# Sample-sequence state updates moved from the scan stage to the out-projection stage, with their operands kept in DRAM

## The chip, the cores and the metric

The kernel runs on one core of a Trainium2 chip. The metric is the device time of one execution in microseconds (us). The engines are named as in the profile: PE (TensorE, matrix multiplies; PEld are its weight loads), DVE (VectorE), ACT (ScalarE), POOL (GpSimd) and SP (SyncE, which here only issues DMAs). Each engine works through its own list of instructions in order: an instruction that waits holds everything behind it on that engine.

## The reference

One inference step of a small hybrid decoder, for one prompt of 512 tokens and 8 sampled sequences of 4 new tokens each (544 tokens in all, width 1024). There are two layers. Layer A is a Mamba-2 mixer: an in-projection, a causal convolution, a chunked state-space scan and an out-projection. Layer B is a dilated attention mixer over keys and values shared with a cache. What the change concerns is the state of the sampled sequences in layer A:

```python
def step(s, inp):
    dec, cs = inp
    return dec[..., None, None] * s + cs, s

s_final, s_in = lax.scan(step, s0, (chunk_decay, chunk_states))
y_off = jnp.einsum("bctgn,cbgjpn,bgjct->bctgjp", Cc, s_in, jnp.exp(a_cs))
y = (y_diag + y_off).reshape(b, lp, nh, p)[:, :l]
return y, s_final.reshape(b, nh, p, SSM_STATE)
```

For each of the 8 sampled sequences and each of the 32 heads the old state (64 x 128 fp32, the input `state_ssm`) is used twice: the output `y_off` multiplies it with C, and the new state is decay x old state + B^T (x dt decay), which is an output of the step (`ssm_sample`). All the old states are 8.4 MB, and so are all the new ones. Nothing later in the step reads a new state; it only has to be stored. The output `y` goes on into the gate and the out-projection.

## The kernel before

Matrix multiplies are fp32-accurate: each operand is split into a high and a low part (`whi`/`wlo`, `xh`/`xl`, `vh`/`vl`, `hh`/`hl`), and three passes are summed in PSUM. A projection tile makes 128 output features of all 544 tokens; `pa` holds tokens 0 to 255 of it and `pb` the other 288. Work is emitted in program order and a list scheduler sets each engine's order from it; `tc.high_priority` pulls single instructions ahead.

**Stage A (0 to about 375 us).** The in-projection tiles are a filler that `run(pace)` deals out between the scan's units. The 4 groups of 8 heads have six units each: `ssm_chunk(g, c)` for the prompt's four chunks of 128 tokens and `ssm_quad(g, q)` for two sets of four sampled sequences (the "quads"; Q0 to Q7 in order of group and set). A unit is a generator in two or three parts, so that one unit's operand preparation stands ahead of the part of the unit before that uses it. `ssm_quad` does:
- `s0`: two loads of 512 KB (two sequences each, 128 x 1024) into `s_t`, from a pool of two such buffers, on SP's queue (L685);
- `cbp`, `xp`, `yos`: PE transposes B and x, and multiplies C with the old state (`yos`, four matmuls);
- `xdt`, `xdd`: x times dt, and x times dt and decay, 128 x 512, on DVE;
- `btr`, `xr`: B and `xdd` as high and low parts in different rows of one tile, by `hi_lo_rows` (one ACT at L213 and one DVE at L214 each);
- L723, on POOL: the old state times its decay `dec`, in place, 128 x 512 per sequence;
- `ms`, `yds`, `yot`, `ytmp`: the output of the new tokens, added into `v`;
- `update(j)`: one matmul `up` (K = 32 rows) per sequence, DVE adds it to the decayed state (L744), and after each second sequence ACT's queue stores 512 KB (`ssmS`, L746).

At the end of a group `gate_skip` adds the skip term to `v` and `gate_mul_a` multiplies `v` by the gate `uz` (L592, on POOL for groups 0 to 2 and on DVE for the last) and sums squares (`ssq`, L598). `v_split` then makes `vh` and `vl` of it (L757 ACT, L758 DVE).

**Middle stage (about 375 to 600 us).** The out-projection has 8 tiles, m = 0 to 7, of 96 matmuls each. After a tile's matmuls `h1_tile(m)` scales, adds the residual, makes `hh` and `hl`, squares on ACT (`sqb`) and adds the squares into `hss`, on POOL for m = 1 to 6 (L861). Then one step of the generator `tables` follows, which makes the attention's bias tables: a PE matmul `bvp` per step, whose one-hot operand `oh` comes by DMAs from POOL's queue. After the out-projection come 16 tiles for the shared keys and values (`wkv`), 48 matmuls each. The weights of a tile come in halves (`wraw`, 512 KB each) and are split into `whi` on ACT (L199) and `wlo` on DVE (L200) about a tile ahead.

**Slabs.** Tiles of 128 x 4 x 544 fp32 (8.7 KB a partition) come by `half(...)` from one pool of 13 buffers. In the out-projection 12 are held: four each of `vh` and `vl`, two each of `hh` and `hl`.

**Stage C (about 600 to 963 us)** is the attention, which the change leaves alone.

Of the kernel before, what the change touches and what calls it, by code (L numbers as in the profile page):

```python
# [12 lines left out]
F32 = mybir.dt.float32  # L13
# [14 lines left out]
HP = 64  # L28
NG = 4
# [95 lines left out]
def tile_yoco_step(  # L125
# [16 lines left out]
    def mm(*a, **k):  # L142
        pin(nc.tensor.matmul(*a, **k))  # L143
# [16 lines left out]
    def pss(name, shape=(128, 512)):  # L160
        return psum.tile(list(shape), F32, name=name, tag="ss", bufs=5)
# [50 lines left out]
    def hi_lo_rows(out, src, c, rows=128):  # L212
        nc.scalar.activation(out, src, AF.Copy, scale=hls[0:rows, c + 1:c + 2])  # L213
        nc.vector.scalar_tensor_tensor(out, src, hls[0:rows, c:c + 1], f32(out), op0=ALU.mult, op1=ALU.add)  # L214
# [68 lines left out]
    sed0 = dram.tile([128, 2, 8], F32, name="sed0")  # L283
    sed = dram.tile([2, NH, 32], F32, name="sed")
    vnd = dram.tile([NB, TS, ATH, 128], F32, name="vnd")
    kvd = dram.tile([ATH, 128, T + SEQ], F32, name="kvd")

    def dap(t, off, ap):
# [204 lines left out]
    def spread_decays():  # L493
        dx = pss("dx")
        mm(dx[:, 0:384], ones, dgs.rearrange("p a b -> p (a b)"), start=True, stop=True)
        dv = dx[:, 0:384].rearrange("p (r j h) -> p r j h", r=3, j=4)
        nc.scalar.copy(dec[:, 0:4], dv[:, 0])
        nc.scalar.copy(dec[:, 4:12].rearrange("p (j r) h -> p r j h", r=2), dv[:, 1:3])

    def tok_transposes():  # L500
        spread_decays()
# [38 lines left out]
    def bc(ap, n):  # L540
        return ap[:, :, None].to_broadcast([ap.shape[0], ap.shape[1], n])
# [121 lines left out]
    def ssm_quad(g, q):  # L663
        xs, v, G = xs_t[g], v_t[g], grp[g]
        hs = slice(8 * g, 8 * g + 8)
        if q == 0:
            bp = wk.tile([128, 2, 4, 32], F32, name="bp", bufs=1)
            cp = wk.tile([128, 2, 4, 32], F32, name="cp", bufs=1)
            nc.gpsimd.memset(bp, 0.0)
            thrice(bp.rearrange("p q j c -> p (q j) c"), BT[:, g, SEQ:T])  # L670
            nc.gpsimd.memset(cp, 0.0)
            nc.gpsimd.tensor_copy(cp.rearrange("p q j c -> p (q j) c")[:, :, 0:TS],
                                  CT[:, g, SEQ:T].rearrange("p (b c) -> p b c", c=TS))
            as_ = wk.tile([128, 8, 32], F32, name="as", bufs=1)
            dma(as_, dap(sed, 8 * g * 32, [[0, 128], [32, 8], [1, 32]]))
            es = wk.tile([128, 4, 32], F32, name="es", bufs=1)
            for s in range(2):
                dma(es[64 * s:64 * s + 64], dap(sed, (NH + 8 * g + s) * 32, [[0, 64], [64, 4], [1, 32]]))
            G["smp"] = bp, cp, as_, es
        bp, cp, as_, es = G["smp"]  # L680
        sq_ = slice(16 * q, 16 * q + 16)
        s_t = []
        for jp in range(2):
            s_t.append(wk.tile([128, 2, 512], F32, name="s0", bufs=2))
            dma(s_t[jp], s0[g, :, 4 * q + 2 * jp:4 * q + 2 * jp + 2, :])  # L685
        xpd = wk.tile([128, 4, 4, 32], F32, name="xpd", bufs=1)
        nc.gpsimd.memset(xpd, 0.0)
        for i in range(4):
            thrice(xpd[:, i], xs[:, i, SEQ + 16 * q:SEQ + 16 * q + 16])
        bq = bp[:, q].rearrange("p a b -> p (a b)")  # L690
        cbp = pss("cbp")
        transpose(cbp[:, 128:256], bq, ident)
        mm(cbp[:, 0:16], bq, CT[:, g, SEQ + 16 * q:SEQ + 16 * q + 16], start=True, stop=True)
        xp = pss("xp", (128, 4, 128))
        for i in range(4):
            transpose(xp[:, i, :], xpd[:, i].rearrange("p a b -> p (a b)"), ident)
        yo = pss("yos")
        for j in range(4):
            mm(yo[32 * j:32 * j + 32, :], cp[:, q, j, :], s_t[j // 2][:, j % 2, :], start=True, stop=True)
        bt = wk.tile([128, 128], F32R, name="btr", bufs=1)  # L700
        hi_lo_rows(bt, cbp[:, 128:256], 0)
        cbm = wk.tile([128, 16], F32, name="cbs")
        with tc.high_priority():
            nc.vector.tensor_tensor(cbm, cbp[:, 0:16], smask, op=ALU.mult)
        yos = wk.tile([128, 512], F32, name="yos", bufs=1)
        nc.scalar.copy(yos, yo)
        xph = xp.rearrange("p a (h d) -> p (a h) d", d=HP)
        xdt = wk.tile([128, 8, HP], F32, name="xdt", tag="xd", bufs=3)
        with tc.high_priority():
            nc.vector.tensor_tensor(xdt, xph, bc(tok[:, 4 + q, 1, hs], HP), op=ALU.mult)  # L710
        xdd = wk.tile([128, 8, HP], F32, name="xdd", tag="xd", bufs=3)
        with tc.high_priority():
            nc.vector.tensor_tensor(xdd, xph, bc(tok[:, 4 + q, 2, hs], HP), op=ALU.mult)
        xr = wk.tile([128, 8, HP], F32R, name="xr", bufs=1)
        hi_lo_rows(xr, xdd, 2)
        ms = wk.tile([128, 8, 16], F32, name="ms")
        nc.vector.tensor_tensor(ms, as_[:, :, sq_], bc(tok[:, 4 + q, 0, hs], 16), op=ALU.subtract)
        nc.vector.tensor_scalar(ms, ms, 0.0, None, op0=ALU.min)
        nc.scalar.activation(ms, ms, AF.Exp)
        nc.vector.tensor_tensor(ms, ms, cbm[:, None, :].to_broadcast([128, 8, 16]), op=ALU.mult)  # L720
        for j in range(4):
            sv = s_t[j // 2][:, j % 2, :].rearrange("p (a b) -> p a b", b=HP)
            nc.gpsimd.tensor_tensor(sv, sv, bc(dec[:, 4 + 4 * q + j, hs], HP), op=ALU.mult)  # L723
# [12 lines left out]
        nc.vector.tensor_tensor(v[:, :, SEQ + 16 * q:SEQ + 16 * q + 16], yds,  # L736
                                tmp.rearrange("p i j t -> p i (j t)"), op=ALU.add)

        def update(j):
            up = pss("up", (128, 8, HP))  # L740
            mm(up.rearrange("p a b -> p (a b)"), bt[32 * j:32 * j + 32, :],
               xr[32 * j:32 * j + 32].rearrange("p a b -> p (a b)"), start=True, stop=True)
            sv = s_t[j // 2][:, j % 2, :].rearrange("p (a b) -> p a b", b=HP)
            nc.vector.tensor_tensor(sv, up, sv, op=ALU.add)  # L744
            if j % 2:
                nc.scalar.dma_start(ssmS[g, :, 4 * q + j - 1:4 * q + j + 1, :], s_t[j // 2])  # L746

        for j in range(3):
            update(j)
        yield  # L750
        update(3)

    def v_split(g, i):
        gg = g_gate[:, 4 * g + i:4 * g + i + 1]
# [89 lines left out]
    def h1_tile(m, pa, pb):  # L844
# [15 lines left out]
        nc.scalar.activation(sq, hm, AF.Square)  # L860
        (nc.gpsimd if m < KD - 1 else nc.vector).tensor_tensor(hss, hss, sq, op=ALU.add)  # L861

    def load_out(m):
        return [load_w(w_out[m, :, 0:8, :]), load_w(w_out[m, :, 8:16, :])]

# [55 lines left out]
    for m in range(KD):  # L921
        w = nxt
        pa, pb = pj("pa"), pj("pb")
        if m == 0:
            full(pa, w, v_h, v_l, 0, HA, 0, 12)
            full(pb, w, v_h, v_l, HA, T, 0, 12)
            full(pa, w, v_h, v_l, 0, HA, 12, 15)
            full(pb, w, v_h, v_l, HA, T, 12, 15)
            ms_add(ms, ssq, inv_i, True, True)
            full(pa, w, v_h, v_l, 0, HA, 15)  # L930
            full(pb, w, v_h, v_l, HA, T, 15)
            nxt = load_out(1)
# [12 lines left out]
        h1_tile(m, pa, pb)  # L945
        next(tables, 0)


    vsn = wk.tile([32, ATH, 128], F32, name="vsn", bufs=1)
# [27 lines left out]
    for i, (f, h, wi) in enumerate(order):  # L977
# [30 lines left out]
        prev = f(h, pa, pb)  # L1008
        next(prev)
        next(tables, 0)  # L1010
        if i == 8:
            dma(vnd[:].rearrange("b t h d -> (b t) h d"), vsn)

# [591 lines left out]
```

## Time and profile before

| | |
|---|---|
| median of 3 runs | 964.43 us (963.14 to 966.48) |
| profiled execution | 964.79 us |
| its span, first to last instruction | 963.0 us |
| mean granted TensorE clock | 0.982 |
| PE busy | 932.9 us, 97% of the span |
| DVE, ACT, POOL busy | 682.2, 482.1, 200.5 us |
| DMA | 168.49 MB, 175 GB/s on average |

The profile describes one execution. A row of a group of instructions reads: line, engine, operation, output<-input by the program's names, count, then the shortest, median and longest duration in ns, the first and last start in us, and the shape. In the rows of waits the columns are the total time waited, how often, and the longest. A row of a stretch of time gives each engine's busy time and, behind it, the number of instructions, then PEclk (the granted clock as a share of full speed), the busy share of the DMA engines and GB/s. "DMA to landing" is the time from a DMA's issue to its end. In the chain of waits, one row is a piece of the chain that led to the stretch's end: start, length, what it was.

### The profile page before, as it was taken

How to read it: one execution, taken by the hardware profiler on the slowest of the kernel's cores; microseconds unless marked ns; L12 is line 12 of the kernel's file. 1: busy time of each engine (PE TensorE's matmuls, PEld its weight loads, DVE VectorE, ACT ScalarE, POOL GpSimd, SP SyncE). 2: the span in 40 equal slices, each digit the busy share in tenths (PEclk: the TensorE clock that was granted, in tenths of full speed). 3: DMA queues.
4: the chain of work that ended last, by engine and by line, in shares of the span. 5: the costliest groups of instructions: out<-in, count | busy, mean ns of one | idle time of the engine just before them, and what ended most of it. 6: DMA issues, size and time to landing. Idle time of an engine off the chain costs nothing.

```text
span 963.0 us, 21807 instructions
## 1 busy us (share of the span) xinstructions
PE 932.9 (97%) x8645; PEld 847.5 (88%) x8645; DVE 682.2 (71%) x1435; ACT 482.1 (50%) x1057; POOL 200.5 (21%) x295
## 2 busy tenths in 40 slices
PE   7999998999999998999999999999999999989996
PEld 5999987889788888999999999888888888868896
DVE  6687979998998798555597347767667766757532
ACT  5558745654645654322354214555555555555542
POOL 3232545544544532111010000000000000000021
PEclk9999999899999999999999999999999999989898
DMA  7252355255366432545386556775876876844411
GB/s 259 83 157 74 120 201 190 78 166 180 130 194 205 160 114 95 154 139 194 117 272 188 197 180 188 257 251 181 271 234 197 266 264 208 276 163 158 143 45 50
DMA packets 75934, 168.49 MB, mean 175 GB/s; under 512 B 19446, under 2 KB 37192, under 8 KB 75320
## 3 DMA queue, kind: packets, MB, share of 16 engines
q1 hardware_dynamic: 71880, 154.91, 49.0%
q10 hardware_dynamic: 2880, 9.44, 2.5%
q0 software_dynamic: 1072, 2.74, 1.1%
q8 instruction: 68, 1.11, 0.5%
q14 instruction: 34, 0.28, 0.1%
HBM read 141.14 MB, written 25.93 MB: 173 GB/s over the span
## 4 chain that ended last, share of the span: by engine, by line
PE 88%; DVE 5%; DMA 3%; ACT 1%; POOL 1%; issue 1%; DVEq 0%; SPq 0%; ACTq 0%
PE pa L143 34%; PE pb L143 30%; PE sp L143 3%; PE so L143 3%; PE pv L143 2%; PE s L143 2%; PE yd L143 1%; PE ptp L146 1%; PE w L146 1%; PE csp L143 1%; PE yo L143 1%; DMA m<-aed 1%; PE xp L146 1%; DMA kc<-ck 1%; PE yos L143 1%; DVE vl L758 1%
## 5 line engine op out<-in xcount | busy, mean ns | idle before, releaser
L199 ACT ACTIVATE whi<-wraw 128x1024 fp32r<-128x1024 f32 x72 | 76.2, 1058 | 99.6 <-PE pb L143 66.2
L200 DVE TENSOR_TENSOR wlo<-wraw,whi 128x1024 fp32r<-128x1024 f32 x71 | 88.9, 1252 | 50.5 <-ACT whi L199 50.5
L143 PE MATMUL pa<-bq,whi 128*128 128x272 f32 x512 | 103.1, 297 | 0.0
L143 PE MATMUL pa<-xh,whi 128*128 128x256 f32 (+1 forms) x320 | 92.7, 293 | 3.3 <-ACT xh L365 3.3
L143 PE MATMUL pb<-xh,whi 128*128 128x288 f32 (+1 forms) x304 | 90.4, 299 | 3.9 <-ACT cb L331 3.9
L143 PE MATMUL pb<-xl,whi 128*128 128x288 f32 (+1 forms) x304 | 91.2, 302 | 0.9 <-DVE xl L368 0.8
L143 PE MATMUL pa<-xl,whi 128*128 128x256 f32 (+1 forms) x320 | 90.8, 287 | 0.9 <-DVE xl L368 0.8
L143 PE MATMUL pb<-xh,wlo 128*128 128x288 f32 (+1 forms) x304 | 87.4, 299 | 0.0
L143 PE MATMUL pa<-xh,wlo 128*128 128x256 f32 (+1 forms) x320 | 85.0, 283 | 0.0
L143 PEld LDWEIGHTS pa<-bq,whi 128*128 128x128 f32 x512 | 81.9, 190 | 0.9
L143 PE MATMUL pb<-bq,whi 128*128 128x272 f32 x384 | 79.9, 302 | 0.3 <-DVE kv L1100 0.2
L143 PE MATMUL pa<-bq,wlo 128*128 128x272 f32 x256 | 74.2, 290 | 0.0
L529 DVE SCALAR_TENSOR_TENSOR co<-cb,cvp,co 128x568 f32<-128x568 f32 x72 | 66.6, 925 | 1.2 <-ACT co L527 0.2
L143 PEld LDWEIGHTS pa<-xh,whi 128*128 128x128 f32 x320 | 60.7, 190 | 6.2 <-ACT xh L365 3.7
L143 PEld LDWEIGHTS pb<-bq,whi 128*128 128x128 f32 x384 | 62.5, 194 | 1.7 <-DVE qpad L1091 0.7
L143 PEld LDWEIGHTS pa<-xl,whi 128*128 128x128 f32 x320 | 60.6, 189 | 3.4 <-DVE xl L368 1.4
L143 PEld LDWEIGHTS pb<-xl,whi 128*128 128x128 f32 x304 | 57.8, 190 | 6.5 <-issue 4.4
L143 PEld LDWEIGHTS pb<-xh,whi 128*128 128x128 f32 x304 | 58.0, 191 | 5.0 <-ACT cb L331 4.1
L1332 POOL COPY lse<-mxs 128x1 f32<-128x1 f32 x16 | 3.8, 236 | 273.3 <-DVE mxs L1330 273.3
L143 PEld LDWEIGHTS pa<-xh,wlo 128*128 128x128 f32 x320 | 58.0, 188 | 1.3 <-issue 0.9
L1158 ACT ACTIVATE whi<-wraw 128x512 fp32r<-128x512 f32 x64 | 40.2, 628 | 37.4 <-PE pa L143 17.1
L143 PEld LDWEIGHTS pb<-xh,wlo 128*128 128x128 f32 x304 | 56.6, 190 | 2.2 <-issue 2.2
(378 smaller groups left out, 2786.8 us busy)
## 6 DMA issues: line engine op xcount, KB each, us to landing
wraw<-w_in SPq DMA_DIRECT2D x40, 512.0 KB
kc<-ck SPq DMA_DIRECT2D x32, 640.0 KB
vc<-cv SPq DMA_DIRECT2D x32, 640.0 KB
wraw<-wb SPq DMA_DIRECT2D x32, 512.0 KB
s<-s SPq DMA_DIRECT2D x16, 512.0 KB
m<-aed SPq DMA_DIRECT2D x16, 512.0 KB
ssmS<-s ACTq DMA_DIRECT2D x16, 512.0 KB
wraw<-w_out SPq DMA_DIRECT2D x16, 512.0 KB
```

What stands on the lines that cost most here:

```text
L143: pin(nc.tensor.matmul(*a, **k))
L146: pin(nc.tensor.transpose(*a))
L199: a = nc.scalar.activation(hi, raw, AF.Copy)
L200: b = lo_eng.tensor_tensor(lo, raw, f32(hi), op=ALU.subtract)
L529: nc.vector.scalar_tensor_tensor(o, cb[:, k:k + n], cvp[:, ti, k:k + 1], o, op0=ALU.mult, op1=ALU.add)
L758: nc.vector.scalar_tensor_tensor(v_l[g][:, i, :], v_t[g][:, i, :], gg, f32(v_h[g][:, i, :]), op0=ALU.mult, op1=ALU.subtract)
L1158: nc.scalar.activation(hi, src[p][j], AF.Copy)
L1332: nc.gpsimd.tensor_copy(lse[:, i16:i16 + 1], mx[:, 2:3])
```

## The change

`ssm_quad` keeps the old state's use for `yos`, and no longer makes the new states. It writes what they need to DRAM instead: `xdd` (128 x 512) and a copy of B (`bts`, 128 x 128, copied out of PSUM by ACT) into the new array `sxd`, and once for all quads the decays into `dcd`, all from SP's queue. A new generator `states` makes the new states in the middle stage, quad by quad. The first part of `state_quad(g, q)` issues four DMAs from POOL's queue, loads the old states again (1 MB at once, into columns 0 to 2047 of one slab `sx`), multiplies by the decays on POOL (L865), and makes `btr` and `xr`. The second part does the four `up` matmuls, the four DVE adds (L874) and two stores of 512 KB, which are now on POOL's queue (L876). The B that comes back is put into columns 2048 to 2175 of the same slab. Both parts run after out-projection tiles m = 2 to 7 (Q0 to Q5), and one part each after wkv tiles 2 to 5 (Q6 and Q7).

```diff
@@ ssm_quad
-        bt = wk.tile([128, 128], F32R, name="btr", bufs=1)
-        hi_lo_rows(bt, cbp[:, 128:256], 0)
+        bt = wk.tile([128, 128], F32, name="bts", bufs=2)
+        nc.scalar.copy(bt, cbp[:, 128:256])
+        dma(sxd[g, q, :, 512:640], bt)
...
-        xr = wk.tile([128, 8, HP], F32R, name="xr", bufs=1)
-        hi_lo_rows(xr, xdd, 2)
+        dma(sxd[g, q, :, 0:512], xdd.rearrange("p a b -> p (a b)"))
...
-        for j in range(4):
-            sv = s_t[j // 2][:, j % 2, :].rearrange("p (a b) -> p a b", b=HP)
-            nc.gpsimd.tensor_tensor(sv, sv, bc(dec[:, 4 + 4 * q + j, hs], HP), op=ALU.mult)
...
-        def update(j):
-            up = pss("up", (128, 8, HP))
-            mm(up.rearrange("p a b -> p (a b)"), bt[32 * j:32 * j + 32, :],
-               xr[32 * j:32 * j + 32].rearrange("p a b -> p (a b)"), start=True, stop=True)
-            sv = s_t[j // 2][:, j % 2, :].rearrange("p (a b) -> p a b", b=HP)
-            nc.vector.tensor_tensor(sv, up, sv, op=ALU.add)
-            if j % 2:
-                nc.scalar.dma_start(ssmS[g, :, 4 * q + j - 1:4 * q + j + 1, :], s_t[j // 2])
@@ middle stage
+    def state_quad(g, q):
+        s_ = half("sx").rearrange("p a b -> p (a b)")
+        bs = s_[:, 2048:2176]
+        s_ = s_[:, 0:2048].rearrange("p (j c) -> p j c", j=4)
+        nc.gpsimd.dma_start(s_, s0[g, :, 4 * q:4 * q + 4, :])
+        sx = wk.tile([128, T], F32, name="sx", tag="vt", bufs=2)[:, 0:512]
+        nc.gpsimd.dma_start(sx, sxd[g, q, :, 0:512])
+        dq = wk.tile([128, 4, 8], F32, name="dq", bufs=2)
+        nc.gpsimd.dma_start(dq, dcd[:, g, 4 * q:4 * q + 4])
+        nc.gpsimd.dma_start(bs, sxd[g, q, :, 512:640])
+        for j in range(4):
+            sv = s_[:, j, :].rearrange("p (a b) -> p a b", b=HP)
+            nc.gpsimd.tensor_tensor(sv, sv, bc(dq[:, j], HP), op=ALU.mult)
+        bt = wk.tile([128, 128], F32R, name="btr", bufs=1)
+        hi_lo_rows(bt, bs, 0)
+        xr = wk.tile([128, T], F32R, name="xr", tag="hb", bufs=2)[:, 0:512]
+        hi_lo_rows(xr, sx, 2)
+        yield
+        for j in range(4):
+            up = pss("up")
+            mm(up, bt[32 * j:32 * j + 32, :], xr[32 * j:32 * j + 32, :], start=True, stop=True)
+            nc.vector.tensor_tensor(s_[:, j, :], up, s_[:, j, :], op=ALU.add)
+            if j % 2:
+                nc.gpsimd.dma_start(ssmS[g, :, 4 * q + j - 1:4 * q + j + 1, :], s_[:, j - 1:j + 1, :])
+        yield
...
         h1_tile(m, pa, pb)
         next(tables, 0)
+        if m > 1:
+            next(states, 0)
+            next(states, 0)
...
         next(prev)
         next(tables, 0)
+        if 1 < i < 6:
+            next(states, 0)
```

Where this puts the instructions, at three places.

SP, early in the scan, before. `m<-aed`, `ea<-aed`, `as<-sed` and `es<-sed` are small operands of the scan, `wraw<-w_in` are in-projection weights, and `s_...<-s` are a quad's old states.

```order
L685 DMA s_1677<-s 128x1024
L610 DMA m<-aed 128x1024
L635 DMA ea<-aed 64x4x128 x2
L190 DMA wraw<-w_in 128x1024
L610 DMA m<-aed 128x1024
```

The same place now:

```order
L689 DMA s_2090<-s 128x1024
L719 DMA sxd<-xdd 128x512
L614 DMA m<-aed 128x1024
L639 DMA ea<-aed 64x4x128 x2
L190 DMA wraw<-w_in 128x1024 x2
```

The write of `xdd`, which waits for DVE, now stands ahead of loads that the next prompt chunk needs. The loads of the old states, whose buffers in before came free when the stores of the quad before had landed, now wait only for the `yos` matmuls of that quad.

PE, at the end of the out-projection tile m = 5, before:

```order
L143 MATMUL pb<-vl,whi 128x288
L143 MATMUL pb<-vh,wlo 128x288
L143 MATMUL bvp<-oh,relt 128x504
L143 MATMUL pa<-vh,whi 128x256
L143 MATMUL pa<-vl,whi 128x256
```

And now:

```order
L143 MATMUL pb<-vl,whi 128x288
L143 MATMUL pb<-vh,wlo 128x288
L143 MATMUL bvp<-oh,relt 128x504
L143 MATMUL up<-xr,btr 128x512 x4
L143 MATMUL pa<-vh,whi 128x256
```

The four `up` of a quad stand in one piece behind `bvp` and ahead of the next tile. All of the rest of PE's list is in its old order, with the 32 `up` gone from stage A.

POOL, in the middle of the out-projection (the `hss` rows are those of tiles m = 1 to 6), before:

```order
L876 DMA oh<-ohp 33x1168 x4
L861 TENSOR_TENSOR hss<-hss,sqb 128x544 x3
L876 DMA oh<-ohs 33x1288 x2
L861 TENSOR_TENSOR hss<-hss,sqb 128x544 x3
L876 DMA oh<-ohs 33x1288 x10
```

And now, from the stores of Q1 on (the `hss` rows here are m = 4 and, in the last but two, m = 5):

```order
L850 TENSOR_TENSOR hss<-hss,sqb 128x544
L857 DMA sx<-s 128x2048
L862 DMA sx<-sxd 128x128
L865 TENSOR_TENSOR sx<-sx,dq 128x512 x4
L861 DMA dq<-dcd 128x32
L876 DMA ssmS<-sx 128x1024 x2
L857 DMA sx<-s 128x2048
L862 DMA sx<-sxd 128x128
L865 TENSOR_TENSOR sx<-sx,dq 128x512 x4
L861 DMA dq<-dcd 128x32
L850 TENSOR_TENSOR hss<-hss,sqb 128x544
L876 DMA ssmS<-sx 128x1024 x2
```

The first load here is that of Q2 and the second that of Q3. In the built program Q1, Q2, Q3, Q4 and Q5 all get one and the same slab, so that each of their loads waits until the two stores of the quad before have landed; Q0, Q6 and Q7 get slabs of their own. Q0's and Q1's loads stand well ahead, before the `hss` of m = 1.

More of the change, by code (lines that the diff above doesn't have):

```diff
@@ L285, in tile_yoco_step @@
     vnd = dram.tile([NB, TS, ATH, 128], F32, name="vnd")
+    sxd = dram.tile([NG, 2, 128, 640], F32, name="sxd")
+    dcd = dram.tile([128, NG, 8, 8], F32, name="dcd")
     kvd = dram.tile([ATH, 128, T + SEQ], F32, name="kvd")
@@ L498, in spread_decays @@
         nc.scalar.copy(dec[:, 4:12].rearrange("p (j r) h -> p r j h", r=2), dv[:, 1:3])
+        for g in range(NG):
+            dma(dcd[:, g], dec[:, 4:12, 8 * g:8 * g + 8])
     def tok_transposes():
@@ L737, in ssm_quad @@
                                 tmp.rearrange("p i j t -> p i (j t)"), op=ALU.add)
-        def update(j):
-            up = pss("up", (128, 8, HP))
-            mm(up.rearrange("p a b -> p (a b)"), bt[32 * j:32 * j + 32, :],
-               xr[32 * j:32 * j + 32].rearrange("p a b -> p (a b)"), start=True, stop=True)
-            sv = s_t[j // 2][:, j % 2, :].rearrange("p (a b) -> p a b", b=HP)
-            nc.vector.tensor_tensor(sv, up, sv, op=ALU.add)
-            if j % 2:
-                nc.scalar.dma_start(ssmS[g, :, 4 * q + j - 1:4 * q + j + 1, :], s_t[j // 2])
-        for j in range(3):
-            update(j)
         yield
-        update(3)
     def v_split(g, i):
@@ L861, in h1_tile, with all_states @@
         (nc.gpsimd if m < KD - 1 else nc.vector).tensor_tensor(hss, hss, sq, op=ALU.add)
+    def state_quad(g, q):
[23 more added lines that the diff above has]
+        yield
+    def all_states():
+        for g in range(NG):
+            for q in range(2):
+                yield from state_quad(g, q)
+    states = all_states()
     def load_out(m):
```

## The prediction

> **What bounds the kernel now.** I read the page first, then PE's waits, then the stretches around them.
>
> ```profile
> PE 932.9 (97%) x8645; PEld 847.5 (88%) x8645; DVE 682.2 (71%) x1435; ACT 482.1 (50%) x1057; POOL 200.5 (21%) x295
> ...
> PE 88%; DVE 5%; DMA 3%; ACT 1%; POOL 1%; issue 1%; DVEq 0%; SPq 0%; ACTq 0%
> ```
>
> PE is the bound: 97% busy, 88% of the chain. So the time changes only by what PE executes, waits for, or runs at half clock. PE's waits that touch the moved work:
>
> ```profile
> PE pb L143 <- ACT cb L331: 3.9, 1, 3.9
> ...
> PE pa L143 <- DVE wlo L200: 2.9, 1, 2.9
> ...
> PE yos L143 <- DMA s<-s: 2.0, 1, 2.0
> ...
> PE up L143 <- DVE xdd L627: 0.3, 1, 0.3
> ```
>
> The stretches with these waits, three out-projection tiles, and last the scan as a whole:
>
> ```profile
> core 0: us, PE busy (x) PEld busy (x) DVE busy (x) ACT busy (x) POOL busy (x), PEclk, DMA share, GB/s
> 163.60:167.90 4.30, 0.36 (x5) 0.15 (x3) 4.30 (x4) 1.56 (x4) 4.22 (x3) 0.87 0.84 325
> 167.90:173.60 5.70, 5.70 (x27) 5.35 (x31) 5.41 (x8) 3.52 (x11) 4.71 (x9) 0.50 0.00 0
> 243.70:246.30 2.60, 0.61 (x4) 0.00 (x0) 2.56 (x6) 0.64 (x2) 2.43 (x7) 1.00 0.83 295
> 371.60:374.70 3.10, 0.23 (x2) 0.03 (x1) 3.10 (x4) 0.00 (x0) 0.67 (x1) 1.00 0.00 0
> 374.70:378.40 3.70, 3.67 (x17) 3.67 (x18) 3.67 (x6) 1.30 (x2) 1.14 (x1) 0.54 0.45 142
> ...
> 412.20:424.20 12.00, 12.00 (x97) 12.00 (x96) 6.10 (x9) 3.23 (x4) 1.36 (x1) 1.00 0.34 111
> 424.20:436.50 12.30, 12.30 (x99) 12.26 (x98) 6.21 (x9) 3.42 (x4) 1.36 (x1) 1.00 0.57 200
> 436.50:448.80 12.30, 12.30 (x100) 12.30 (x99) 5.84 (x9) 3.42 (x4) 2.39 (x3) 1.00 0.69 233
> ...
> 75.00:375.00 300.00, 290.86 (x2367) 260.10 (x2366) 267.11 (x424) 176.81 (x386) 142.95 (x192) 0.99 0.45 150
> ```
>
> Three things. In stage A, PE idles about 4 us at 163.7 and 3 us at 371.6, with DVE (and POOL the first time) busy throughout. After each the granted clock falls to 0.50 or 0.54, which costs half of the stretch: 2.9 us of 5.7, 1.7 of 3.7. After 2.6 us at 243.7 it stays at 1.00. And in the out-projection DVE is half idle and POOL nearly free, but PE has no gap at all: a tile takes 12.2 us, and whatever stops PE there is added in full.
>
> **Part 1: what leaves stage A.**
>
> ```profile
> L143 PE MATMUL up<-xr,btr x32: 463/492/501, 116.4 to 358.4; 32*128 32x512 f32 x32
> L744 DVE TENSOR_TENSOR s<-up,s x32: 677/685/693, 119.5 to 359.9; 128x512 f32<-128x512 f32 x32
> ...
> L723 POOL TENSOR_TENSOR s<-s,dec x32: 1039/1067/2123, 101.6 to 346.0; 128x512 f32<-128x512 f32 x32
> ...
> L214 DVE SCALAR_TENSOR_TENSOR xr<-xdd,csts,xr x8: 736/744/1376, 108.3 to 350.9; 128x512 fp32r<-128x512 f32 x8
> ...
> L213 ACT ACTIVATE btr<-cbp,csts x8: 350/364/373, 99.3 to 341.1; 128x128 fp32r<-128x128 f32 x8
> L214 DVE SCALAR_TENSOR_TENSOR btr<-cbp,csts,btr x8: 335/342/350, 101.3 to 342.7; 128x128 fp32r<-128x128 f32 x8
> ...
> L685 SPq DMA_DIRECT2D s<-s x16: 327/328/334, 12.7 to 336.2; - x16
> ...
> 116.42 0.50 PE L143 MATMUL up<-xr,btr 32*128 32x512 f32 x3
> 116.85 0.38 PE L143 MATMUL pa<-xl,whi 128*128 128x256 f32 x1
> ...
> 238.33 4.15 DMA ssmS<-s
> ...
> 242.53 3.74 DMA s<-s
> ...
> 367.43 6.11 DVE vl L758 x4
> 373.54 1.15 DVE wlo L200
> ```
>
> - PE: three `up` in a row hold PE from 116.42 to 116.85, 0.43 us; I estimate the same for a lone fourth, so 0.86 per quad, 8 x 0.86 = 6.9 us gone, and the wait of 0.3.
> - The `yos` wait: the load of 3.74 us begins only when a store of 4.15 has landed. That store is gone from stage A; the load is then released by PE and issued a quad earlier. 2.0 us gone.
> - DVE sheds 32 x 0.685 + 8 x (0.744 + 0.342) = 30.6 us, POOL 32 x 1.067 = 34.1 us. In the stretch at 163.6 both are full. I take 2 of the 3.9 us off, and an idle gap of 2 us is shorter than the 2.6 that kept full clock, so 2.9 more. At 371.6 a DVE backlog ends the wait (`vl` 6.11, then `wlo` 1.15); with the last two quads' 8 adds and `hi_lo` rows gone (about 7.7 us of DVE) I take 2.4 of 2.9 off and the 1.7.
>
> Sum: 6.9 + 0.3 + 2.0 + 2.0 + 2.9 + 2.4 + 1.7 = 18.2; I take 17.6, since a bit of waiting turns up elsewhere. Bounds: 11 (`up`, `yos`, and half of the rest), 23 (all waits gone).
>
> Costed at nothing: the copies `bts` (they replace the `btr` ACT of 0.364, ACT has half its time free), 20 added DMA issues on SP (0.33 us each as for `s<-s`; PE's list of waits has none for a weight's DMA in this stage), and 16 issues that leave ACT. The cover that could go: `sxd<-xdd` waits for DVE ahead of `m<-aed` on SP; if DVE runs late, so do that chunk's loads.
>
> **Part 2: what the middle stage gains.** PE: Q0, Q1, Q6, Q7 and the others' four `up` in a row, 0.43 per quad as above; for Q0, Q1, Q6, Q7 4 x 0.43 = 1.7 us. They should not wait: Q0's and Q1's operands are loaded before the out-projection, Q6 and Q7 have slabs of their own and one part per tile. DVE's adds and `hi_lo` rows, 4 x 0.685 + 0.744 + 0.342 = 3.8 us a quad, lie in the half of its time that is free there.
>
> Q2 to Q5 are different. Rows for the chain:
>
> ```profile
> 424.21 0.39 PE L143 MATMUL bvp<-oh,relt 66*128 66x504 f32 x1
> ...
> 428.09 0.65 ACT L860 ACTIVATE sqb<-h 128x544 f32<-128x544 f32 x1
> ...
> 428.88 1.36 POOL L861 TENSOR_TENSOR hss<-hss,sqb 128x544 f32<-128x544 f32 x1 [10.96 <-ACT sqb L860]
> ...
> L185 POOL DMA_DIRECT2D csts<-cst x1: 737/737/737, 1.3 to 1.3; - x1
> ...
> L876 POOL DMA_DIRECT2D oh<-ohs x12: 507/507/524, 437.1 to 517.1; - x12
> ...
> DMA to landing us min/median/max: 3.1/4.1/6.8
> ```
>
> *Q2.* Its load and its B stand on POOL behind the `hss` add of tile m = 4, which ends 6.0 us after that tile's `bvp` began (424.21 to 430.24, one tile earlier). PE's `up` of Q2 stands right behind the `bvp` and needs `btr`, so B, so that load. From `bvp`: 6.0 + issue 0.74 (the 128-row issue) + landing of 1 MB + B landing 0.35 behind it + `btr` 0.36 + 0.34 + hops 0.3. For 1 MB on POOL's queue there is no row; below, it is the 325 GB/s of the first stretch: 3.2 us; above, two of the 3.74: 7.5. I take 5.7, nearer the longest landing in the table of `oh` (6.8, of a far smaller transfer) than the lower end. Together 13.8, less 0.4 of `bvp` itself: PE stops for 13.4 us. The ACT and DVE of `btr` wait too, with the next tile's `whi` and `wlo` behind them.
>
> *Q3, Q4, Q5.* All in Q2's slab, so load n+1 waits for store n. The loop: issue 0.74 + load 5.7 + four decays 4 x 1.067 = 4.3 + last add 0.7 + two store issues 1.0 + both stores landed. For these two, below 3.2 (1 MB at 325 GB/s), above two of the 4.15, 8.3; I take 5.7. Sum 18.1 us. The `hss` add of 1.36 lies in it twice, delaying by some 0.7 and 0.9. So three rounds take 3 x 18.1 + 1.6 = 55.9 us, against 3 tiles of 12.2 = 36.6 of PE's work: 19.3 us more, with each of the three stops 5 to 7 us long. Longer than 4, so each brings half clock (2.3, the mean of 2.9 and 1.7); the loop's time hides this for all but the last.
>
> The stage: 13.4 + 19.3 + 2.3 + 1.7 = 36.7 us. With the low landings: Q2 10.9, rounds of 13.1, 3 x 13.1 + 1.6 - 36.6 = 4.3, together 19.2. With the high ones: Q2 15.2, rounds of 22.5, 32.5, half clock 2.9, together 52.3.
>
> *A rule weighed.* The rows give no time for a lone transfer on POOL's queue of this size. The Trainium skill, "DMA: Bandwidth & Descriptors", section "Anatomy of one DMA — SWDGE (gpsimd) path", fits such a transfer as 2.0 us plus the bytes at 436 GB/s. An estimate by it is 4.4 us for 1 MB where I took 5.7; Q2 would stop PE 12.1 us, a round, with both stores in the same 4.4, would be 15.5, and the total some 9 us less than mine. No run here shows which; I keep the rows, because the out-projection's own loads run at 111 to 233 GB/s beside it.
>
> **The sum.** Against the profiled 964.8 us (0.4 above the median): 964.8 - 17.6 + 36.7 = 983.9. I say 984. By the bounds, best against best: 964.8 - 23 + 19.2 = 961; worst: 964.8 - 11 + 52.3 = 1006.
>
> **Rivals.** Within 0.3% of 964.4 (961.5 to 967.3) a measurement of this kernel can't tell a change.
> 1. *The forecast*: PE stops at `up` for Q2 to Q5. For it: in-order POOL, one slab, PE with no gap. Against: the landing times are bounded, not seen. 970 to 1003.
> 2. *Only Q2's stop is paid.* If a round takes 12.6 us or less (landings of 3.0 us each), Q3 to Q5 arrive in time: 964.8 - 17.6 + 13.4 + 2.3 + 1.7 = 964.6, no difference. For it: 325 GB/s occurs. Against: there it took 0.84 of the DMA engines' time, and the out-projection's own traffic, 0.34 to 0.69, has to run beside it.
> 3. *Faster.* No stop at all, if B of Q2 lands before the tile ends: 964.8 - 17.6 + 8 x 0.43 = 950.6. It decides where the stage's stops are under stage A's 17.6 us less 3.4; Q2's alone is estimated at 13.4. Against: the order on POOL, which puts `hss` of the same tile ahead of the load.
> 4. *The gain does not come and the decays are slow.* The longest L723 took 2.123 us, twice the median. With that in the middle stage a round is 22.3 us, the stage 49.3; with a gain of only 11: 1003. The Trainium skill, "GPSIMD Engine Reference", section "8. Key points", has GpSimd and VectorE share their SBUF interfaces, which would stretch POOL's operations beside DVE's; the 32 rows here have a median of 1.067 in a scan whose DVE was busy for 267 of 300 us, so the trace speaks for the short one.
> 5. *The change as written does not take place* is excluded: 32 `up` stand in the middle stage in PE's list.
>
> **How the numbers follow.** The forecast 0.72; rival 2 0.07; rival 3 0.08; rival 4 0.13. The predicted time is the forecast's, 984. The low end takes in the low landings with the usual gain, 964.8 - 17.6 + 19.2 = 966; the high end rival 4's 1003 and a little above. Slower is the forecast and rival 4, and nothing of rival 2: 0.85; same 0.07; faster 0.08.
>
> **What would show it.** Right: PE's waits in the changed profile have four long ones of `up` on `btr` (about 13, then 5 to 7 us each) between about 430 and 500 us; the load of `sx` starts when the two stores before it have landed, and the stretches behind the stops show a clock near 0.5. In stage A the waits on `cb`, `wlo` and `s<-s` shrink, and the out-projection starts about 17 us earlier. Wrong: PE's waits of `up` are short; or the out-projection starts no earlier, because a wait on `m<-aed` or `xdd` took the old ones' place; or the loads and stores on POOL's queue take 3 us or 10.

## The result and the profile after

The changed kernel takes 998.16 us (median of four runs, 994.63 to 998.29) against 964.04 us, a ratio of 1.034 (95% interval 1.031 to 1.037): 34 us slower. The forecast was 984 us in a range of 966 to 1004. The profiled execution is the lowest of the four, with a span of 992.9 us; the spans of the other three are 996.3 to 996.5.

The page of the changed kernel: busy time, and the granted clock in 40 slices.

```profile
span 992.9 us, 21917 instructions
...
PE 931.5 (94%) x8645; PEld 849.3 (86%) x8645; DVE 686.7 (69%) x1435; ACT 481.3 (48%) x1065; POOL 226.8 (23%) x343
...
PEclk8999999999999999969889999999999999999998
```

PE executes the same matmuls in the same busy time, 931.5 against 932.9 us, in 30 us more. In slices 18, 20 and 21 the clock is down; they lie between 422 and 521 us, in the out-projection from Q2 on and in the first tiles of the key and value projection. PE's waits in the whole kernel, those that touch the change (total, times, longest):

```profile
PE up L143 <- DVE btr L214: 27.1, 3, 15.5
PE pa L143 <- DVE wlo L200: 4.8, 4, 3.1
...
PE pb L143 <- ACT cb L333: 2.8, 1, 2.8
...
PE vp L146 <- DVE vt L979: 2.0, 1, 2.0
PE xp L146 <- DVE cbm L633: 1.4, 1, 1.4
...
PE xp L146 <- DVE xdd L631: 0.7, 1, 0.7
```

27.1 us of new waits stand at `up`. The wait on the load `s<-s` is gone, that on `cb` has gone from 3.9 to 2.8, that on `wlo` has not shrunk, and `xp` waits anew. POOL's timeline from the `hss` of m = 4 to Q5's load shows what `up` waits for (the bracket gives the idle time before and what ended it):

```profile
431.63 1.32 POOL L850 TENSOR_TENSOR hss<-hss,sqb 128x544 f32<-128x544 f32 x1 [3.06 <-ACT sqb L849]
432.90 0.57 POOL L857 DMA_DIRECT2D sx<-s  x1
...
441.50 4.09 POOL L865 TENSOR_TENSOR sx<-sx,dq 128x512 f32<-128x512 f32 x4 [7.46 <-DMA sx<-s]
...
446.45 1.09 POOL L876 DMA_DIRECT2D ssmS<-sx  x2
451.45 0.53 POOL L857 DMA_DIRECT2D sx<-s  x1 [3.91 <-DMA ssmS<-sx]
...
456.77 5.95 POOL L865 TENSOR_TENSOR sx<-sx,dq 128x512 f32<-128x512 f32 x4 [4.25 <-DMA sx<-s]
...
470.75 0.53 POOL L857 DMA_DIRECT2D sx<-s  x1 [3.45 <-DMA ssmS<-sx]
...
490.68 0.54 POOL L857 DMA_DIRECT2D sx<-s  x1 [6.04 <-DMA ssmS<-sx]
```

This is the loop of one slab: load, decays, stores, landing, load. Its rounds are 18.6, 19.3 and 19.9 us. The stretches in which PE meets it:

```profile
427.00:440.60 13.60, 0.23 (x3) 0.05 (x1) 3.97 (x7) 2.35 (x3) 3.45 (x5) 0.65 0.90 307
440.60:457.70 17.10, 14.96 (x101) 14.53 (x101) 5.86 (x9) 2.58 (x4) 7.75 (x10) 0.78 0.36 130
...
471.00:478.90 7.90, 0.32 (x7) 0.06 (x5) 4.77 (x8) 2.75 (x4) 2.06 (x4) 0.77 0.72 275
...
492.90:497.20 4.30, 0.27 (x3) 0.09 (x1) 0.62 (x2) 1.05 (x2) 1.24 (x2) 0.84 0.84 335
497.20:513.40 16.20, 16.20 (x108) 15.23 (x108) 12.41 (x20) 3.51 (x6) 7.94 (x9) 0.83 0.69 249
```

PE stands still at Q2, Q4 and Q5 while the DMA engines are 0.72 to 0.90 busy; behind each stop the clock is low. At Q3 it does not stop: the tile before it ran at a clock of 0.78 and took so long that the data were there.

All profiled executions on one scale, in us from the span's start: the first `bvp` (end of tile m = 2), the first matmul of the key and value projection, the first of the attention, and the span. The two columns of differences are what the stage in between took. (The attention of the kernel before starts at 580.8 us in its trace, a little earlier than the "about 600" further up.)

| kernel | `bvp` | kv starts | attention starts | span | out-projection from `bvp` | kv projection |
|---|---|---|---|---|---|---|
| before | 411.9 | 473.4 | 580.8 | 963.0 | 61.5 | 107.4 |
| changed | 399.4 | 497.9 | 614.4 | 992.9 | 98.5 | 116.5 |
| no states made | 400.6 | 462.1 | 569.6 | 948.1 | 61.5 | 107.5 |
| `hss` on DVE | 402.0 | 494.1 | 612.2 | 991.7 | 92.1 | 118.1 |
| B early | 401.7 | 487.3 | 608.2 | 987.1 | 85.6 | 120.9 |
| all quads in kv | 401.6 | 463.1 | 598.1 | 1003.1 | 61.5 | 135.0 |
| one slab, halves | 400.7 | 478.1 | 605.5 | 986.5 | 77.4 | 127.4 |
| own slabs | 401.6 | 470.4 | 588.0 | 980.6 | 68.8 | 117.6 |
| no Q6, Q7 | 399.6 | 499.5 | 607.9 | 988.8 | 99.9 | 108.4 |
| decays on DVE | 401.3 | 513.5 | 627.8 | 1005.7 | 112.2 | 114.3 |
| spread, POOL | 401.9 | 467.1 | 590.8 | 968.8 | 65.2 | 123.7 |
| spread, DVE | 401.3 | 468.6 | 590.7 | 969.0 | 67.3 | 122.1 |
| spread, held | 400.2 | 463.6 | 586.2 | 965.6 | 63.4 | 122.6 |

For the change: -12.5 up to `bvp`, +37.0 to the key and value projection, +9.1 in it, and -3.7 in the attention. The last is not the change's: the attention (span less its start) takes 382.2 us in the trace of before and 378.5 in that of the changed kernel, and from 377.9 to 381.0 in the nine other traces of the table in which the attention does not wait for late states. In the trace of before the clock is low for longer there (rows at the end). The other three executions of the changed kernel are about 3.5 us longer than the profiled one, at a granted clock of 0.967 to 0.968 against 0.970, which is worth 3 us at most (an estimate: the lost share of the clock times the span, about 32.5 against 29.8 us); where they lose it is not on record.

### The profile page after: what moved, and what is told of

It is laid out like the page before. It is cut to its first block, busy times and chain, and to the rows that moved or that the text cites. A ratio compares the mean times of both kernels' runs of the same rounds, so it can differ in the third digit from the quotient of the medians.

```text
span 992.9 us, 21917 instructions
## 1 busy us (share of the span) xinstructions
PE 931.5 (94%) x8645; PEld 849.3 (86%) x8645; DVE 686.7 (69%) x1435; ACT 481.3 (48%) x1065; POOL 226.8 (23%) x343
## 5 line engine op out<-in xcount | busy, mean ns | idle before, releaser
L200 DVE TENSOR_TENSOR wlo<-wraw,whi 128x1024 fp32r<-128x1024 f32 x71 | 97.7, 1377 | 59.4 <-ACT whi L199 59.0
L143 PE MATMUL pb<-bq,whi 128*128 128x272 f32 x384 | 77.8, 296 | 1.0 <-DVE qpad L1119 0.7
L533 DVE SCALAR_TENSOR_TENSOR co<-cb,cvp,co 128x568 f32<-128x568 f32 x72 | 61.6, 856 | 1.3 <-ACT co L531 0.2
```

The costliest lines, as they stand in the source:

```text
L200: b = lo_eng.tensor_tensor(lo, raw, f32(hi), op=ALU.subtract)
L533: nc.vector.scalar_tensor_tensor(o, cb[:, k:k + n], cvp[:, ti, k:k + 1], o, op0=ALU.mult, op1=ALU.add)
```

## The experiments

Each is an edit of the changed kernel. The ratio is to the kernel before on the same chip.

**The scan's gain alone.**

```diff
-    states = all_states()
+    states = iter(())
```

> The changed kernel with the middle stage's state work left out: no loads of sx, no up, no stores, so the new states of the sampled sequences are not made. The writes of xdd and B to DRAM stay in the scan. Theory (the loss is the middle stage's stops alone; the scan's gain is what the changed kernel's trace shows, 13.3 us at the start of the out-projection): 964.0 - 13.3 = 951, from 949 to 953; PE's wait on wlo at the end of the scan is still about 3 us. Rival (the move also costs something outside the middle stage's state work, by the added writes or by the other order of loads): 955 or more.

949.36 us (947.98 to 952.29), ratio 0.987 [0.983, 0.990]: 13.6 us faster than before. The theory holds. The scan's gain is real, and out-projection and key and value projection take what they took before. In this run's own trace 11.3 us of the gain stand ahead of `bvp` (400.6 after 411.9); 3.7 us more of the trace's difference lie in the attention, as in the other runs, so part of the 13.6 may not be the scan's. By the table, `bvp` comes 9.9 to 12.5 us earlier in the kernels with this scan, the changed kernel's 12.5 being the most. And all of the loss is the state work in the middle stage: 34.1 us slower with it and 13.6 faster without, 47.7 us together, where its matmuls are worth 3.4.

**POOL's order.**

```diff
-        (nc.gpsimd if m < KD - 1 else nc.vector).tensor_tensor(hss, hss, sq, op=ALU.add)
+        nc.vector.tensor_tensor(hss, hss, sq, op=ALU.add)
```

> The changed kernel with the hss adds on DVE instead of POOL, nothing else. Theory (POOL's order sets Q2's stop; behind hss the next thing ahead of Q2's load is the pair of oh issues, which waits for bvp): Q2's load starts 1.5 us after bvp and not 5.9 us after it, Q2's stop falls from 13.5 to about 9 us, the loop from Q2 to Q5 keeps its rounds of 18 to 19 us, total 992 to 995. Rival (the stop is set by the slab's release, the landing of Q1's stores, and hss is beside it): stop 12 us or more, total 997 to 999.

993.32 us, ratio 1.032 [1.029, 1.035]. The expectation took 13.5 us for Q2's stop; the changed kernel's row says 15.5. It fell by 4.4 us:

```profile
PE up L143 <- DVE btr L214: 19.4, 2, 11.1
```

That is the 4.3 us by which Q2's load no longer waits for `hss`. Theory confirmed in place and size: an add that nobody waits for held a load that PE waited for.

**B's place.**

```diff
-        bs = s_[:, 2048:2176]
+        bs = wk.tile([128, 128], F32, name="bs", bufs=1)
+        nc.gpsimd.dma_start(bs, sxd[g, q, :, 512:640])
         ...
-        nc.gpsimd.dma_start(bs, sxd[g, q, :, 512:640])
```

> The changed kernel with B loaded into a small tile of its own, ahead of the 1 MB load and not behind it, nothing else. Theory (the slab's loop is the limit, and B behind the load is only where PE meets it): PE no longer waits at up, but DVE's adds wait for the loaded and decayed state with the next tiles' wlo behind them, so that the waits come back as PE pa or pb on wlo; the loads stay 18 to 19 us apart; total 985 to 998. Rival (B's place behind the load is the whole cause, the adds have slack): no stop over 2 us in the out-projection, total 953 to 960.

989.50 us, ratio 1.028 [1.024, 1.032], inside the theory's range. PE's stops at `btr` are gone and others stand in their place:

```profile
PE up L143 <- DVE sx L874: 9.2, 11, 3.4
```

Now the matmuls of a quad wait one by one for the adds of those before (their PSUM), and the adds for the decays and the 1 MB load. Of the out-projection's 37 us 13 came back, and the key and value projection lost 4.4 more; the loads of Q2, Q3 and Q4 stay 22.2 and 18.5 us apart. So where PE meets the loop is a small part, and the loop the larger. Even that part is not B's place alone: in this run Q5's load starts 2.4 us after Q4's, released by a matmul (`pb`) and not by a landing, so Q5 left the loop as well.

**A shorter loop.**

```diff
-        nc.gpsimd.dma_start(s_, s0[g, :, 4 * q:4 * q + 4, :])
+        for jp in range(2):
+            nc.gpsimd.dma_start(s_[:, 2 * jp:2 * jp + 2, :],
+                                s0[g, :, 4 * q + 2 * jp:4 * q + 2 * jp + 2, :])
```

> The changed kernel with one slab kept for all quads and the old states loaded in two halves of 512 KB, each half released by the store of that half; B's load then stands ahead of the states' loads. To be compared with the run with B early (989.5 us, loads 22.2 and 18.5 us apart). Theory (PE and DVE are held by the loop load, decays, adds, stores, landing): a shorter loop gives the time back; one half's load overlaps the other's landing, rounds of 14 to 16 us, still over the 12.2 of a tile: total 975 to 985. Rival (DVE's or POOL's own order holds PE, whatever the loop): 987 to 992, as with B early.

986.40 us, ratio 1.024 [1.021, 1.027]: too slow for the theory, and at the rival's edge. The out-projection fell from 85.6 to 77.4 us, but what it saved the key and value projection mostly gave back (127.4 after 120.9; here Q6 and Q7 share the slab too). From one quad's first half to the next one's, the rounds from Q1 to Q5 came to 18.2, 18.7, 17.7 and 15.7 us, hardly shorter, because both stores of a quad still stand behind all four decays on POOL. Not decided by this run.

**Away from the one slab.** All quads in the key and value projection, one part per tile:

```diff
-        if m > 1:
-            next(states, 0)
-            next(states, 0)
...
-        if 1 < i < 6:
-            next(states, 0)
+        next(states, 0)
+        if i == 15:
+            next(states, 0)
```

> The changed kernel with all eight quads placed in the 16 tiles of the key and value projection, one part per tile, where the eight slabs of vh and vl are free; nothing in the out-projection. Theory (one slab is what makes the loop): no load waits for a store's landing, up costs 8 x 0.43 = 3.4 us, total 951 + 3.4 = 954, up to 962 if single loads come late. Rival (traffic is the limit: 18 MB more in some 116 us that already move 205 GB/s, 360 GB/s together): PE waits there for weights too, total 970 or more.

1005.50 us, ratio 1.046 [1.042, 1.049]: both expectations miss the cause. No load waits for a landing, and the out-projection is back at 61.5 us, but two new waits come:

```profile
PE pa L143 <- ACT bq L1060: 17.8, 3, 10.4
PE up L143 <- DVE xr L214: 15.8, 4, 5.8
```

The copy of `xdd` uses the two buffers of the values' output tiles (`vt`, `kt`), and its load stands behind the stores on POOL's queue; the last quads then hold up the attention's first operands `bq`. In that stage PE waits on no weight.

**Buffers of their own.** Q0 and Q1 as they were, Q2 to Q7 in the key and value projection:

```diff
+        if own:
+            o_ = half("so").rearrange("p a b -> p (a b)")[:, 0:640]
+            nc.gpsimd.dma_start(o_, sxd[g, q])
+            sx, bs = o_[:, 0:512], o_[:, 512:640]
...
+    late = [state_quad(g, q, True) for g in range(1, NG) for q in range(2)]
```

> Q0 and Q1 in the out-projection as in the changed kernel, Q2 to Q7 in the tiles of the key and value projection, with xdd and B in a slab of their own (one DMA) and not in the buffers that the values' output tiles use, and with every load issued two to four tiles ahead of up. Theory (in the run with all quads there, 1005.5 us, PE waited on xr, whose operand shared two buffers with vt and kt and whose load stood behind stores on POOL; at the end the late quads held the attention's first operands): without the sharing no wait over 1 us, 949.4 + 8 x 0.43 + about 2 for Q0 = 955, from 952 to 960. Rival (too much traffic there): 970 or more, with PE waiting on weights or on xr's load as before.

980.83 us, ratio 1.018 [1.015, 1.021]. The wait on `xr` is gone, as said, and the number is still missed by 21 us. By the table, the out-projection takes 7.3 us more than without states, the key and value projection 10.1 and the attention 14.1. Of the last, 10.7 us is PE waiting on `bq` at its start (8.4 on ACT, 2.3 on DVE), with a low clock behind. On `wlo` PE waits for 1.7 us in the middle stage; its other 3.5 are in the scan, much as without states (3.3).

**Q6 and Q7.**

```diff
-        if 1 < i < 6:
-            next(states, 0)
```

> The changed kernel without Q6 and Q7 (their new states are not made); Q0 to Q5 as they are. The key and value projection took 116.5 us in the changed kernel and 107.5 without any states. Theory (2.0 us of PE waiting on vt behind a held btr, the half clock after it, and 0.9 for up are Q6's and Q7's; the half clock after Q5's stop is Q5's): it takes 110 to 112 us, total 992 to 995. Rival (all of the 9 us comes from Q5's stop and stores, Q6 and Q7 lie beside): 996 to 998.

991.12 us, ratio 1.029 [1.025, 1.032]; the key and value projection takes 108.4 us against 116.5. Below the theory's range because Q5 stopped PE for only 0.3 us in this run, so that its half clock is missing as well (in the changed kernel a clock of 0.85 over the first 15.5 us of that stage, 2.3 us). That leaves about 5.8 us for Q6 and Q7, where 0.9 was forecast.

What Q6 does is in the changed kernel's timelines of DVE and POOL:

```profile
515.26 3.96 DVE L214 SCALAR_TENSOR_TENSOR btr<-sx,csts,btr 128x128 fp32r<-128x128 f32 x1 [1.22 <-ACT btr L213]
519.14 0.44 DVE L979 TENSOR_TENSOR vt<-pb,rstd 128x288 f32<-128x288 f32 x1
...
527.33 5.23 DVE L200 TENSOR_TENSOR wlo<-wraw,whi 128x1024 fp32r<-128x1024 f32 x1
```

```profile
515.01 4.05 POOL L865 TENSOR_TENSOR sx<-sx,dq 128x512 f32<-128x512 f32 x4
...
527.42 4.05 POOL L865 TENSOR_TENSOR sx<-sx,dq 128x512 f32<-128x512 f32 x4
```

A `btr` of 0.34 us takes 3.96 and ends with the fourth decay; a `wlo` of 1.22 takes 5.23 beside the next four. PE's 2.0 us on `vt` are behind that `btr`.

**Decays on DVE.**

```diff
-            nc.gpsimd.tensor_tensor(sv, sv, bc(dq[:, j], HP), op=ALU.mult)
+            nc.vector.tensor_tensor(sv, sv, bc(dq[:, j], HP), op=ALU.mult)
```

> The changed kernel with the decays (L865) on DVE instead of POOL, nothing else. In the changed kernel's trace four decays take 4.1 us when DVE waits and 5.9 to 6.4 when it works, wlo takes 2.06 instead of 1.22 us beside them, and one btr of 0.34 us lasted 3.96 us and ended with the fourth decay. Theory (POOL's decay and a DVE operation with two SBUF inputs hold each other up; this makes the waits around Q0 and Q6): the tile with Q0 falls from 14.6 to 13 us or less, the key and value projection from 116.5 to 111 to 113, a round of the loop by 1.5 to 3 us, total 982 to 990. Rival (they do not hold each other up, the long rows are waits for something else): 996 or more, since DVE gets 22 us more work in order.

1010.26 us, ratio 1.048 [1.045, 1.051]: the wrong way, in the rival's range. Yet half of the theory is confirmed: the tile with Q0 falls from 14.6 to 13.0 us, no `wlo` of the middle stage takes more than 1.23 us, PE's wait on `vt` is gone, and all `btr` are short again (the columns are the shortest, median and longest ns):

```profile
L214 DVE SCALAR_TENSOR_TENSOR btr<-sx,csts,btr x8: 338/342/347, 395.8 to 551.8; 128x128 fp32r<-128x128 f32 x8
```

The rest was misjudged. On DVE the four decays stand ahead of `btr` and wait for the load, so PE's stops at `up` grow to 40.0 us, and the rounds to 19.0, 23.2 and 22.0. The key and value projection takes 114.3 us, little under 116.5: Q5 now stops PE for 7.7 us, with 5.3 us of the stage at half clock behind it, and one wait of 1.3 on the load of `oh` is new.

**Spread.** A quad per two out-projection tiles (Q0 to Q3), Q4 to Q7 in the first nine tiles of the key and value projection with every operand in slabs of their own, B early:

```diff
+    AT_OUT = {1: (0, 0), 2: (0, 1), 3: (1,), 4: (1, 2), 5: (2,), 6: (2, 3), 7: (3,)}
+    AT_KV = {1: (3,), 2: (4, 6), 3: (4,), 4: (5, 7), 5: (5,), 6: (6,), 7: (6,), 8: (7,), 9: (7,)}
```

> The changed kernel with the quads spread: a quad per two tiles of the out-projection (Q0 to Q3, one slab each in turn, so that a round of 18 to 19 us has 24.4 us), Q4 to Q7 in the first nine tiles of the key and value projection with all their operands in slabs of their own; B in a tile of its own ahead of the states; decays on POOL. Theory (the loss is the loop's stops, and then what the decays do to DVE): no wait of PE on btr or xr over 1 us, attention not late, but about 1 to 2 us a quad by wlo beside the decays: 949.4 + 3.4 + 8 to 16 = 961 to 969. Rival (traffic or DVE's order costs it wherever it stands): 975 or more, as with the slabs of its own (980.8).

> As the spread quads, with the decays on DVE. Theory: without the decays on POOL nothing holds wlo up: 949.4 + 8 x 0.43 + 1 to 5 = 954 to 958, faster than the kernel before. Rival (DVE has no room for 22 us more beside the projections): slower than the spread quads with decays on POOL.

972.00 us (ratio 1.008 [1.005, 1.011]) and 970.32 us (1.007 [1.005, 1.009]); the two don't differ. The pace takes away the loop's stops: from `bvp` the out-projection takes 65.2 and 67.3 us, and the attention starts on time. The forecasts of 961 to 969 and 954 to 958 are missed by the key and value projection, 123.7 and 122.1 us. With the decays on POOL, PE waits 2.4 us on `hl` and 2.1 on `vt` there, with the clock at 0.50 for 6.8 and 3.4 us behind. With the decays on DVE, one wait is the largest, and ACT's own timeline shows why: its rows for Q4 to Q7 were put ahead of `whi` and `bsr` and wait there for their loads. First PE's wait, then ACT's rows:

```profile
PE up L143 <- ACT bsr L944: 6.7, 3, 5.4
...
483.48 1.01 ACT L213 ACTIVATE so<-so,csts 128x128 fp32r<-128x128 f32 x2 [3.96 <-DMA so<-sxd]
...
489.51 0.40 ACT L213 ACTIVATE so<-so,csts 128x128 fp32r<-128x128 f32 x1 [4.40 <-DMA so<-sxd]
489.82 1.04 ACT L199 ACTIVATE whi<-wraw 128x1024 fp32r<-128x1024 f32 x1
490.77 0.25 ACT L944 COPY bsr<-bs 128x132 f32<-128x132 f32 x1
```

**Spread, with that order kept.** The rows and decays of Q4 to Q7, and the key and value projection's `whi` and `wlo`, are held in the order in which they are written; the decays are on DVE, and these quads begin about two tiles later:

```diff
-            return split_w(raw, both, lo_eng)
+            return split_w(raw, both, lo_eng, fixed)
...
-        hi_lo_rows(bt, bs, 0)
-        hi_lo_rows(xr, sx, 2)
+        hi_lo_rows(bt, bs, 0, keep=own)
+        hi_lo_rows(xr, sx, 2, keep=own)
```

> As the spread quads with decays on DVE (970.3 us), but the hi and lo rows and decays of Q4 to Q7 are kept behind the whi and wlo of the tile that is emitted before them, and these quads begin two tiles later. In the run before, ACT's hi and lo rows of Q4 to Q7 stood ahead of whi and bsr and waited there for their loads (up to 4.4 us at a time), with PE behind. Theory (that order is what is left of the loss): no wait of PE over 1 us in the key and value projection, which takes 109 to 112 us instead of 118.5, last out-projection tile 12.3 instead of 16.8: 954 to 959, faster than the kernel before. Rival (DVE's room or the traffic): 964 or more.

969.69 us (ratio 1.007 [1.004, 1.010]), the rival's range. ACT's waits for these loads are gone and the out-projection is at 63.4 us, but the held order made one new stop:

```profile
PE pa L143 <- DVE wlo L200: 6.7, 1, 6.7
```

In the first tile of the key and value projection `wlo` now stands behind the last tile's `h` and Q3's decays on DVE; that tile's first part takes 14.4 us where it took 5.3 without states. Without these 9.1 us this version would be at about 960.6, beside the kernel before (962.3 on that chip); that is an estimate and wasn't run. No version beat the kernel before.

**The scan's end.** Beside buffers of their own, the four `vl` of group 2 on POOL:

```diff
+        if g == 2:
+            nc.scalar.activation(v_t[g][:, i, :], v_t[g][:, i, :], AF.Copy, scale=gg)
+            nc.gpsimd.tensor_tensor(v_l[g][:, i, :], v_t[g][:, i, :], f32(v_h[g][:, i, :]), op=ALU.subtract)
+            return
```

> As the run with slabs of their own, and the four vl of group 2 on POOL (ACT scales, POOL subtracts) instead of DVE. One vl fewer stands ahead of the wlo for which PE waits 3.1 us at the end of the scan. Theory (that wait is DVE's order there, not its load: a block of vl stands ahead of the wlo): the wait shrinks to 1 to 2.3 us, the half clock behind it goes, total 1.5 to 4 us less than with slabs of their own. Rival (the wait is set by when the last gate products come): no change within 1 us.

986.97 us, ratio 1.026 [1.022, 1.029], 6.1 us slower than without (980.83) where 1.5 to 4 less was expected. The longest wait on `wlo` is still 3.0 us, and PE now waits 5.6 us on `whi` (1.7 without), which ACT makes. What ends that wait is not settled.

## Why the prediction was right, and where its sizes were off

The direction, the mechanism and the place were right; the time was 14 us short, and the measured 998.2 lies nearer to rival 4's 1003 than to the forecast's 984. By its steps:

- *Part 1, 17.6 us.* 12.5 at `bvp` in the changed kernel's trace, 9.9 to 12.3 in the other runs' (11.3 without states, where the time fell by 13.6). Right: `up` and the `yos` wait. Mis-sized: at 163.7 the wait went from 3.9 to 2.8, not to 1.9, and the clock still fell (0.50 in a stretch of 2 us). Wrong: the wait on `wlo` at the scan's end, of which 2.4 us and the half clock were taken off, is 3.1 after 2.9. It was taken for a backlog of DVE that gets shorter; less work on DVE did not shorten it. Missed: `xp` waiting 2.1 us on DVE's `cbm` and `xdd`.
- *Q2's stop, 13.4 us.* 15.5. `hss` ended 6.0 us after `bvp` as forecast. The load was the term that was off: 8.6 us from issue to the first decay instead of 0.74 + 5.7, in a stretch whose DMA engines were 0.90 busy.
- *The loop, 55.9 us for three rounds.* 57.8. The terms, from POOL's timeline: 5.3 to 6.9 from a load's issue to its decays, decays 4.1 to 6.0, 4.0 to 6.6 from the last store's issue to the next load. Some terms were too large and some too small, and that the sum came out so near is partly luck. PE met less of it: from Q2's `up` to Q5's it took 54.5 us, three tiles of 12.3 and 17.6 more, where 19.3 more were forecast. That the stops would be three of 5 to 7 us was wrong in their spread (0, 7.6, 4.0), since the half clock behind Q2's stop let Q3 be in time.
- *The out-projection, 13.4 + 19.3 + 0.9 = 33.6 up to the key and value projection.* 37.0, or 3.4 more: 2.1 at Q2's stop, 2.1 in the two tiles with Q0 and Q1 (27.6 us, where two of before take 24.6 and 0.9 was forecast; the waits on `wlo` beside Q0's decays are 1.1 of it), 0.9 for Q5's own `up` and the end of its tile, and 1.7 less in the loop.
- *Q6 and Q7, "they should not wait".* This step failed: 9.1 us in their stage, where 2.3 of half clock (Q5's) and 0.9 of `up` were forecast. About 5.8 of it are Q6's and Q7's, by the run without them. The price missed is the decays' hold on DVE, rival 4's mechanism: PE's 2.0 us on `vt` and the low clock behind it (0.50 and 0.72 in two stretches of 2 us, some 1.6 us) come with the held `btr` and go with the decays on DVE. What makes up the remaining 1 to 2 us is not shown. The prediction had spoken against that mechanism by the median of 1.067 us of POOL's rows; but it is DVE's rows that show it, and there not as a slower rate: 3.96 for 0.34. The Trainium skill, "SBUF — State Buffer", section "SBUF: two separate sides", calls the shared ports an exclusive lock which the loser waits out. The trace agrees, and shows more: DVE was kept out for all four decays. It was not always DVE that lost: two other sets of four decays took 5.9 us instead of 4.1 (456.8 and 496.0), with a `wlo` of 2.07 beside each of them.
- *The rule weighed.* By the Trainium skill's "DMA: Bandwidth & Descriptors", section "Anatomy of one DMA — SWDGE (gpsimd) path", an estimate for 1 MB is 4.4 us. The four loads of 1 MB between 430 and 500 us had a median of 6.0 from issue to landing (5.7 was taken):

```profile
sx<-s POOLq DMA_DIRECT2D x4, 1024.0 KB, 6.0
```

- *Rivals 2 and 3* needed rounds of 12.6 us or no stop; the rounds were 18.6 to 19.9. (Rival 2's sum was a little short of its own condition: three rounds of 12.6 and the 1.6 of `hss` are 2.8 us over three tiles.)

## What to carry to other kernels

Before work is moved into a stage where PE has no gap, follow its buffer: with one buffer, load, compute, store and landing make a round, and if the round is longer than the tile that pays for it, PE pays the rest, however idle the engines are. Then read each in-order queue for what a late load would hold: here an add on POOL, a `btr` on DVE, a `whi` on ACT and an output tile's buffer each turned a free move into a stop, and taking one away showed the next. A gain in one stage (13.6 us) says nothing of the price in the other; measure them apart by leaving the moved work out.

## What the runs showed of the hardware that was not expected

DVE can be shut out by POOL for several instructions in a row (3.96 us for 0.34 and 5.23 for 1.22, above; 0.34 and 1.22 again with the decays off POOL).

And the clock's gate is not a matter of the length of the idle time alone. After PE's wait of 2.0 us in the key and value projection it fell to half; in the attention, after a wait of 2.2 us for `kc` it fell in the kernel before, and after 2.0 us at the same place it did not in the changed one. Nor is it the longer of two waits that decides: at that place it fell after 2.11 us in the run with B early (0.50 over the next 3.4 us), and did not after 2.28 us in the run with the decays on DVE (1.00). First the key and value projection of the changed kernel, then the attention of before, then that of the changed one:

```profile
517.40:520.00 2.60, 0.62 (x5) 0.39 (x4) 2.60 (x3) 0.00 (x0) 1.66 (x2) 0.94 1.07 408
520.00:522.00 2.00, 2.00 (x11) 1.94 (x10) 1.31 (x2) 0.73 (x2) 0.00 (x0) 0.50 1.02 420
```

```profile
859.00:863.00 4.00, 3.60 (x25) 1.64 (x22) 0.61 (x1) 0.52 (x2) 0.00 (x0) 0.59 0.19 75
```

```profile
893.00:897.00 4.00, 3.57 (x36) 2.44 (x33) 1.13 (x5) 0.90 (x3) 0.18 (x1) 1.00 0.15 60
```

The Trainium skill, "TensorE: Matmul & The Clock Gate", section "What's actually happening", has the clock halve after an idle window of about 3.4 us that runs freely. That it runs freely would fit rows that differ by where the gap lies; that shorter gaps of 2.0 and 2.2 us are enough is not in it, and the rows show it. By the rows, such a low clock can come or not come at one and the same place of unchanged work, so a few us of difference between two traces need not be an edit's doing.
